# Two blocks of the per-layer input projection moved between the first products of gate and up, with one more tick before a norm

## The chip, the cores and the metric

The kernel runs on one core of a Trainium2 chip. The metric is the device time of one execution in microseconds (us), as a median of several runs. A core has TensorE (PE, matrix products; PEld is its loading of weights), VectorE (DVE), ScalarE (ACT), GpSimd (POOL) and SyncE (SP, which issues most of the transfers between the chip's memory and the core's own). Each engine works through its own list of instructions and waits on semaphores for the others.

## The reference, cut to what matters

The model has two layers over 512 tokens with 1024 channels. Around the change, each layer does this:

```
merged = ga * (ya @ w_br_a) + gb * (yb @ w_br_b) + gc * (yc @ w_br_c)
x = x + merged @ w_o
h = rmsnorm(x, norm_ffn)
x = x + (silu(h @ w_ffn_gate) * (h @ w_ffn_up)) @ w_ffn_down
h = rmsnorm(x, norm_ple)
x = x + sigmoid(h @ w_ple_gate) * (p[i] @ w_ple_in)
```

The change is about `p[i] @ w_ple_in`, the layer's input: `p[i]` is 512 tokens by 256 channels and depends on nothing computed before, so its product may be made at any point of the layer.

## The kernel before, in words

Everything is kept transposed: 128 channels on the partitions, 512 tokens along a row. Each fp32 operand is split into a high and a low part (`split`, L163: ScalarE copies the high part in L144, VectorE subtracts it in L158), and each product is three matmuls (`mm3`, L176: lines L178, L179, L180). `gemm` (L182) makes one block of 128 output channels and fetches its weights through `weights` (L167), whose buffers `wr`, `wh` and `wl` are three each.

The order of TensorE's work is the order in which the program is written. The other engines' orders are made by the framework's scheduler from the program's order, priorities and estimated durations; `weights` and the first loads of the feed-forward stage are given a higher priority, so that they are placed earlier.

Work that is to run a little later on TensorE is written as a generator. `chunk` (L116) counts products of 128 by 128 (three matmuls each, or six of half width in the feed-forward stage), and every fourth one is a tick, at which the waiting generators take a step. `norm` (L207) is such a generator: after `waits[0]` ticks it transposes the sums of squares on TensorE (L214), VectorE reduces them, POOL takes the power, and after `waits[1]` more ticks TensorE turns the result into rows (L227), which ScalarE copies out (`spread`, L255). `main_norm` (L249) starts one; `rows` (L231) then releases what waits for the norm (`ready`, L121).

The stages of a layer that the change touches:

- **Gates and input blocks** (`layer`, L414). The gates of the convolution branch, m = 4 to 7, are made by `gate_b`; between them `input_block` (L1149) makes the first six of the eight blocks of the layer's input: `inputs` (L1138) loads `pT` and splits it into `e` buffers, each block is two products, ScalarE copies it to a `t` buffer, and SP stores it to the memory `pis`. The convolution's last steps are a generator that runs meanwhile; `merge_b` (L745) then reads its result `conv_qk`.
- **w_o** (L865). Eight blocks of the output product, added to x; `halves_in` and `halves_out` build seven combinations of half operands for the next stage (`wo_h`, `wo_qk`, `wo_v`).
- **Gate and up** (`gate_up`, L936). Eleven steps; each makes two blocks of gate and two of up with seven products, called a11, a12, s1, s2, s3, s4 and a22, each 24 matmuls of 256 columns. They share three PSUM banks: x (`ffn_sc`), y (`ffn_tr`) and z (`ffn_av`). Bank x takes a11, s2, s3 and a22 one after the other, each added to what stands in it, and ScalarE copies the bank out between them (`after`, L981, to `ffn_pt` or `ffn_y`). In step 0 the first three products are begun without their last quarter, which needs the last block of w_o; `third` then begins s1, finishes all three and starts their copies. The weights' split for an item (`prep`, `parted`) is written three items ahead.
- **Down** (`down`, in three parts) and, at its end, `main_norm(st[0])` in `ffn` (L1093), with ticks (2, 2).
- **ple** (L1163). For each block m the gate's product, then `rest` multiplies it with the layer's input: for m below `EARLY` (6) read back from `pis` by `embedded`, for m = 6 and 7 of layer 0 made on the spot by `gemm` into `ple_sc` with operands that `inputs` loads just ahead. Layer 1 makes its last two blocks in another way, in `final`, from the same operands. After layer 0's ple the next layer begins with `glu`, whose first two blocks are made as a pair.

Of the kernel before, what the change touches and what calls it, by code (L numbers as in the profile page):

```python
# [12 lines left out]
F32R = mybir.dt.float32r  # L13
I32 = mybir.dt.int32
AF = mybir.ActivationFunctionType
# [5 lines left out]
P = 128  # L21
L = 2
# [4 lines left out]
KD = 8  # L27
# [22 lines left out]
WARM = 10  # L50
BG = dict(glu=2, natten=3, diff=1, gatec=2, branchc=1, gateb=5, mergea=4, mergea2=2)
FIRST = (["v"] * 4 + ["pt"] * 2 + ["y", "b"], ["y"] * 5 + ["pt"] * 2 + ["b"])
EARLY = 6
GAP = 144
AHEAD = dict(sums=12, loads=10)
BACC = dict(dynamic_dma_scratch_size=1024)
# [6 lines left out]
class Net:  # L63
# [350 lines left out]
    def layer(self, i, h, xsrc, xs):  # L414
        self.i, self.h = i, h
        zs, cs = [], []
        self.todo = self.taps(zs, cs)
        self.glu(zs)
        if i == 0:
            self.lambdas()  # L420
        yc, ya, yb = [], [], []
        sn, sd = {}, {}
        self.natten_in(0, sn, yc)
        self.drain(self.renorm)
        self.h = self.hs
# [12 lines left out]
        self.diff_in(3, sd, ya)  # L438
        for m in range(1, KD):
            self.gate_c(acc, m)  # L440
        for m in range(2):
            self.gate_b(gb, m, AF.Copy, None)
        for g in acc + gb:
            self.act(g, g, AF.Sigmoid, table="sigmoid")
        self.branch_c(acc, yc)
        for m in range(2, 4):
            self.gate_b(gb, m, AF.Sigmoid, "sigmoid")
        self.merge_a(ya, acc)
        conv = self.run(self.conv(cs, yb))
        pairs = self.inputs()  # L450
        for m in range(4, KD):
            self.gate_b(gb, m, AF.Sigmoid, "sigmoid")
            for n in ((0, 1), (2,), (3, 4), (5,))[m - 4]:
                self.input_block(pairs, n)
        self.drain(conv)
        mg = self.merge_b(yb, acc, gb)
        x, h = self.w_o(mg, xsrc)
        h = self.ffn(h, x)
        return self.ple(h, x, xs, self.inputs())

    def proj(self, col0, tag="mm"):
        if self.first:
# [399 lines left out]
        self.stt(es[0], es[1], m[:, 5:6], es[0], ALU.mult, ALU.add)  # L862
        return es[0]

    def w_o(self, mg, xsrc):  # L865
        self.phase = "wo"
        xs, st = [], []
        ts = [None] * KP
        for m in range(KD):
            if m % 2 == 0:  # L870
                two = self.parts_of("x", [512], 2)
            xo = two[m % 2]
            self.nc.sync.dma_start(xo, xsrc[m])
            if m == 0:
                both = [self.ps("mm") for _ in range(2)]
                self.pair(both, self.a["w_o"][self.i, 0:2], mg)
            if m < 2:
                ps = both[m]
            else:
                ps = self.ps("mm")  # L880
                self.gemm(ps, self.a["w_o"][self.i, m], mg)
            self.tt(xo, xo, ps, ALU.add)
            if m == KD - 1:
                self.sumsq(m, xo, st)
            if m % 2 == 0:
                ts[m // 2] = self.halves_in(m // 2, xo)
            else:
                self.halves_out(ts[m // 2], xo)
            if m < KD - 1:
                self.sumsq(m, xo, st)  # L890
            xs.append(xo)
        self.main_norm(st[0])
        return xs, [t["out"] for t in ts]

# [38 lines left out]
        self.follow(self.tt(lo, raw, hi.bitcast(F32), ALU.subtract), "dve")  # L933
        return hi, lo

    def gate_up(self, step, ts, mids):  # L936

        nc, w = self.nc, self.a["w_gu"][self.i, step]
        raw, ops, out = {}, {}, {}

        def load(name, src, plus=None, tag="wr"):
            r = raw[name] = self.sb(tag, [P, 1024])
            nc.sync.dma_start(r, src)
            if plus is not None:
                nc.gpsimd.dma_start(r, plus, accum_op=ALU.add)

        def sums():
            load("s1", w[1, 0], w[1, 1], "e" if step % 2 else "kh")
            load("s3", w[1, 0], w[0, 0], "e")

        def loads():
            load("a11", w[0, 0])
            load("a12", w[0, 1])
            load("a22", w[1, 1])

        def prep(name):  # L960
            def fn():
                for s, p, q in (("s2", "s1", "a11"), ("s4", "s2", "a12")):
                    if name == s:
                        raw[s] = self.sb("rp", [P, 1024])
                        self.follow(self.tt(raw[s], raw[p], raw[q], ALU.add), "dve")
                ops[name] = self.parted(raw[name])
            return fn

        def run(bank, name, j, kps=range(KP), first=False):
            if bank not in out:  # L970
                out[bank] = self.ps(dict(x="sc", y="tr", z="av")[bank], (P, 2, 256))
            self.product(out[bank], ops[name], ts, j, kps, first)

        def outputs():
            g = [self.sb("y" if step % 2 else "pt", [P, 2, 512]) for _ in range(2)]
            for u in range(2):
                for v in range(2):
                    out[u, v] = g[u][:, :, 256 * v:256 * v + 256]
            out["g"] = g

        def after(name):  # L981
            if name == "a11":
                outputs()
                self.mark["act"] = self.act(out[0, 0], out["x"], AF.Copy)
            elif name == "a12":
                self.mark["dve"] = self.tt(out[0, 0], out[0, 0], out["y"], ALU.add)
            elif name == "s2":
                self.mark["act"] = self.act(out[0, 1], out["x"], AF.Copy)
            elif name == "s1":
                self.mark["act"] = self.act(out[1, 1], out["z"], AF.Copy, scale=-1.0)  # L990
            elif name == "s3":
                self.mark["dve"] = self.tt(out[1, 1], out[1, 1], out["x"], ALU.subtract)
            elif name == "s4":
                self.mark["dve"] = self.tt(out[0, 1], out[0, 1], out["z"], ALU.add)
                mids[2 * step] = self.mid(2 * step, out["g"][0])
# [12 lines left out]

        order = [("x", "a11", 0), ("y", "a12", 1), ("z", "s1", 3), ("x", "s2", 2), ("x", "s3", 4),
                 ("z", "s4", 6), ("x", "a22", 5)]  # L1010
        if step:
            order[2:4] = order[3:1:-1]
        items = [[prep(o[1]), use(*o)] for o in order]
        if step == 0:
            def third():
                begin(*order[2])()
                for o in order[:3]:
                    run(*o, (KP - 1,))
                    after(o[1])
            items[0][1], items[1][1], items[2][1] = begin(*order[0]), begin(*order[1]), third  # L1020
        return [({0: sums, 4: loads}.get(n), p, u) for n, (p, u) in enumerate(items)]

    def follow(self, i, engine):
# [66 lines left out]
        self.ready(done)  # L1090
        return md

    def ffn(self, ts, x):  # L1093
        self.phase = "ffn"
        i = self.i
        st, hn, mids, items = [], [], {}, []
# [10 lines left out]

        for p, (first, end) in enumerate(PARTS):
            for n in range(first, end):
                items += self.gate_up(n, ts, mids)  # L1110
            items += self.down(p, mids, lambda m, ps, p=p: done(p, m, ps))
        self.mark = {}
        loads = []
# [13 lines left out]
        for n, (_, _, use) in enumerate(items):  # L1127
# [4 lines left out]
            if n + 3 < len(items):  # L1132
                items[n + 3][1]()
                self.p0 = self.tc.cur_priority
        self.main_norm(st[0])
        return hn

    def inputs(self):  # L1138
        self.phase = "pin"
        pairs = []  # L1140
        for k in range(2):
            r = self.sb("t", [P, 512])
# [2 lines left out]
            self.split(hi, lo, r)  # L1145
            pairs.append((hi, lo))
        return pairs

    def input_block(self, pairs, m):  # L1149

# [12 lines left out]
    def ple(self, h, x, xs, pairs):  # L1163
# [3 lines left out]
        hn, st = [], []  # L1167
        for m in range(KD - 2 * last):
            g = self.sb("t", [P, 512])
            if m < EARLY:  # L1170
                pi = self.embedded(m)
            if m != 1:
                pg = self.ps("mm")
# [12 lines left out]
            self.ready(gate)  # L1186
            if last and m == 3:
                self.gains()
            if m >= EARLY:
                pi = self.ps("sc")  # L1190
                self.gemm(pi, self.a["w_pi"][i, m], pairs)

            def rest(m=m, pi=pi, g=g):
                self.tt(g, g, pi, ALU.mult)
                self.tt(x[m], x[m], g, ALU.add)
# [241 lines left out]
```

## Time and profile before

| | us |
|---|---|
| median of 3 runs (lowest to highest) | 1801.88 (1801.6 to 1803.25) |
| the profiled execution | 1801.18 |
| its span, first to last instruction | 1799.4 |
| TensorE busy in the span | 1780.7 |
| VectorE busy | 1380.7 |
| ScalarE busy | 893.1 |
| POOL busy | 64.1 |

The granted TensorE clock is 0.998 of full speed over the span. In the timeline each row gives a start, a length, the engine, the line, the operation with the tile that it writes and those that it reads, and in brackets the engine's idle time before it with what ended that. Matmuls are pipelined: those of 512 columns are listed 0.39 us long but start 0.23 us apart, those of 256 columns 0.28 us long and 0.12 us apart. So a stretch in which TensorE lost time is best read from the starts.

### The profile page before, as it was taken

Reading aid. Unit: us, or ns where it says so; the run is one execution under the profiler, and the core shown is the slowest. Engines: PE = TensorE matmul, PEld = TensorE weight load, DVE = VectorE, ACT = ScalarE, POOL = GpSimd, SP = SyncE. Lnnn points to the kernel's source line nnn. Section 1 sums busy time; section 2 is a strip of 40 time slices with the busy share of each in tenths; the row PEclk is TensorE's granted clock in tenths of the full one; section 3 lists DMA queues with packets and bytes.
Section 4 is the critical chain, followed back from the end, with each engine's and each line's share of the span. In section 5 each row is a group of like instructions: output and inputs, shape, how many; then the busy total and the mean of one; then the engine's idle time right before and its main releaser. Section 6 shows DMA issues by size and latency. Waiting matters only on the chain. (4 is left out here: it accounts for less than half of the span.)

```text
span 1799.4 us, 27361 instructions
## 1 busy us (share of the span) xinstructions
PE 1780.7 (99%) x10404; PEld 1573.4 (87%) x10404; DVE 1380.7 (77%) x2140; ACT 893.1 (50%) x1495; POOL 64.1 (4%) x102
## 2 busy tenths in 40 slices
PE   9999999999999999999999999999999999999998
PEld 7888888888889899898888888888888998998987
DVE  7878887897877577577777878878887775765776
ACT  5467455325565245255545755553255552543554
POOL 0000000000001000000000000000000100000000
PEclk9999999999999999999999999999999999999999
DMA  5566561325646466253437656523374662764432
GB/s 199 165 189 164 150 161 42 103 91 177 198 111 187 138 155 186 81 145 115 157 123 188 187 153 161 128 62 100 97 225 129 156 186 82 192 175 112 115 109 94
DMA packets 98099, 255.98 MB, mean 142 GB/s; under 512 B 12976, under 2 KB 18480, under 8 KB 97968
## 3 DMA queue, kind: packets, MB, share of 16 engines
q1 hardware_dynamic: 90480, 229.62, 41.8%
q0 software_dynamic: 6336, 23.07, 7.3%
q8 instruction: 82, 1.34, 0.3%
q10 hardware_dynamic: 1152, 1.55, 0.3%
q14 instruction: 49, 0.40, 0.1%
HBM read 215.39 MB, written 7.34 MB: 124 GB/s over the span
## 5 line engine op out<-in xcount | busy, mean ns | idle before, releaser
L144 ACT ACTIVATE ffn_wh<-ffn_wr 128x1024 fp32r<-128x1024 f32 (+1 forms) x114 | 117.3, 1029 | 184.9 <-PE ffn_mm L179 101.8
L161 DVE SCALAR_TENSOR_TENSOR conv_z<-glu_z,pre_par,conv_z 128x512 f32<-128x512 f32 x240 | 179.5, 748 | 2.9
L158 DVE TENSOR_TENSOR ffn_wl<-ffn_wr,ffn_wh 128x1024 fp32r<-128x1024 f32 (+1 forms) x114 | 135.0, 1184 | 47.2 <-ACT ffn_wh L144 46.7
L1040 PE MATMUL ffn_sc<-wo_h,ffn_wh 128*128 128x256 f32 x704 | 130.8, 284 | 4.4 <-ACT ffn_pt L144 4.4
L1040 PEld LDWEIGHTS ffn_sc<-wo_h,ffn_wh 128*128 128x128 f32 x704 | 110.1, 192 | 5.8 <-ACT ffn_pt L144 5.3
L1040 PE MATMUL ffn_sc<-wo_h,ffn_wl 128*128 128x256 f32 x352 | 99.6, 283 | 0.0
L178 PE MATMUL ffn_mm<-ffn_z,ffn_wh 128*128 128x512 f32 x240 | 93.4, 389 | 0.0
L179 PE MATMUL ffn_mm<-ffn_z,ffn_wh 128*128 128x512 f32 x240 | 93.4, 389 | 0.0
L180 PE MATMUL ffn_mm<-ffn_z,ffn_wl 128*128 128x512 f32 x240 | 93.4, 389 | 0.0
L158 DVE TENSOR_TENSOR ffn_t<-ffn_mm,wo_r 128x512 f32<-128x512 f32 x48 | 33.1, 689 | 70.6 <-PE ffn_mm L180 70.6
L158 DVE TENSOR_TENSOR ffn_wl<-ffn_rp,ffn_wh 128x1024 fp32r<-128x1024 f32 x44 | 53.8, 1223 | 30.1 <-ACT ffn_wh L144 30.1
L144 ACT ACTIVATE mergea_wh<-mergea_wr 128x1024 fp32r<-128x1024 f32 (+1 forms) x32 | 27.1, 846 | 96.8 <-PE mergea_mm L179 70.8
L1040 PEld LDWEIGHTS ffn_sc<-wo_h,ffn_wl 128*128 128x128 f32 x352 | 67.5, 192 | 0.0
L1040 PE MATMUL ffn_sc<-wo_qk,ffn_wh 128*128 128x256 f32 x352 | 67.1, 283 | 0.0
L1040 PE MATMUL ffn_sc<-wo_v,ffn_wh 128*128 128x256 f32 x352 | 67.1, 283 | 0.0
L1040 PE MATMUL ffn_av<-wo_h,ffn_wh 128*128 128x256 f32 x352 | 65.3, 283 | 0.0
L144 ACT ACTIVATE ffn_wh<-ffn_rp 128x1024 fp32r<-128x1024 f32 x44 | 46.4, 1055 | 30.6 <-PE ffn_mm L179 17.5
L1040 PEld LDWEIGHTS ffn_sc<-wo_qk,ffn_wh 128*128 128x128 f32 x352 | 54.9, 192 | 0.0
L1040 PEld LDWEIGHTS ffn_av<-wo_h,ffn_wh 128*128 128x128 f32 x352 | 54.9, 192 | 0.0
L1040 PEld LDWEIGHTS ffn_sc<-wo_v,ffn_wh 128*128 128x128 f32 x352 | 54.9, 192 | 0.0
L180 PEld LDWEIGHTS ffn_mm<-ffn_z,ffn_wl 128*128 128x128 f32 x240 | 45.1, 188 | 9.5
L178 PEld LDWEIGHTS ffn_mm<-ffn_z,ffn_wh 128*128 128x128 f32 x240 | 45.1, 188 | 9.2
(666 smaller groups left out, 5786.4 us busy)
## 6 DMA issues: line engine op xcount, KB each, us to landing
ffn_wr<-w_gu SPq DMA_DIRECT2D x66, 512.0 KB, 4.3
ffn_e<-w_gu SPq DMA_DIRECT2D x32, 512.0 KB, 3.6
ffn_e<-w_gu POOLq DMA_DIRECT2D x32, 512.0 KB, 7.8
ffn_wr<-w_fd SPq DMA_DIRECT2D x32, 512.0 KB, 4.5
natten_wr<-w_in SPq DMA_DIRECT2D x16, 512.0 KB, 4.3
natten_b<-bias SPq DMA_DIRECT2D x32, 256.0 KB, 2.9
diff_wr<-w_in SPq DMA_DIRECT2D x16, 512.0 KB, 3.7
gatec_wr<-w_in SPq DMA_DIRECT2D x16, 512.0 KB, 3.8
```

The source lines that it names most:

```text
L144: i = self.nc.scalar.activation(out, in_, func, **kw)
L158: return self.nc.vector.tensor_tensor(out, a, b, op)
L161: return self.nc.vector.scalar_tensor_tensor(out, a, s, b, op0, op1)
L178: mm(out, wh, ah, start=first, stop=False)
L179: mm(out, wh, al, start=False, stop=False)
L180: mm(out, wl, ah, start=False, stop=last)
L1040: mm(bank[:, u], w[:, u, kp], t, start=begin and n == 0, stop=False, skip_group_check=True)
```

## The change

- In step 0 of gate and up, one block of the layer's input is made after `third` (that is, after a11, a12 and s1) and another after s2. They use an `mm` bank, ScalarE copies each one out, and SP stores it to `pis`. Layer 0 makes its blocks 6 and 7 there, layer 1 its blocks 4 and 5.
- Their operands are loaded and split during w_o, after its blocks 1 and 2: twice `pT` (into `a` and `b` buffers) and twice a block of `w_pi` (into `r` and `a` buffers).
- In layer 1 the gates m = 4 to 7 of the convolution branch are followed by one input block each (0, 1, 2, 3), six blocks before. Layer 0 keeps its order.
- ple reads every block from `pis`; its two products on the spot are gone, and layer 0 no longer calls `inputs` ahead of it.
- The norm behind down gets ticks (3, 2).

```diff
-EARLY = 6
...
         for m in range(4, KD):
             self.gate_b(gb, m, AF.Sigmoid, "sigmoid")
-            for n in ((0, 1), (2,), (3, 4), (5,))[m - 4]:
+            for n in (((0, 1), (2,), (3, 4), (5,)), ((0,), (1,), (2,), (3,)))[i][m - 4]:
                 self.input_block(pairs, n)
         self.drain(conv)
         mg = self.merge_b(yb, acc, gb)
-        x, h = self.w_o(mg, xsrc)
-        h = self.ffn(h, x)
-        return self.ple(h, x, xs, self.inputs())
+        extra = self.extra_inputs(range(6 - 2 * i, 8 - 2 * i))
+        x, h = self.w_o(mg, xsrc, extra)
+        h = self.ffn(h, x, extra)
+        return self.ple(h, x, xs, self.inputs() if i == L - 1 else None)
...
             xs.append(xo)
+            if m in (1, 2):
+                extra["pair"](m - 1)
         self.main_norm(st[0])
...
                 for o in order[:3]:
                     run(*o, (KP - 1,))
                     after(o[1])
-            items[0][1], items[1][1], items[2][1] = begin(*order[0]), begin(*order[1]), third
+                extra["block"](0)
+
+            def fourth():
+                use(*order[3])()
+                extra["block"](1)
+
+            items[0][1], items[1][1] = begin(*order[0]), begin(*order[1])
+            items[2][1], items[3][1] = third, fourth
...
-        self.main_norm(st[0])
+        self.main_norm(st[0], (3, 2))
...
+    def extra_inputs(self, ms):
+        nc, i = self.nc, self.i
+        pairs, blocks = [None, None], {}
+
+        def pair(k):
+            ph, self.phase = self.phase, "pin"
+            r = self.sb("t", [P, 512])
+            nc.sync.dma_start(r, self.a["pT"][i, k])
+            hi, lo = [self.sb("ab"[k], [P, 512], F32R) for _ in range(2)]
+            self.split(hi, lo, r)
+            pairs[k] = hi, lo
+            w = self.sb("t", [P, 256])
+            nc.sync.dma_start(w, self.a["w_pi"][i, ms[k]])
+            hi, lo = self.sb("a" if k else "r", [P, 256], F32R), self.sb("r", [P, 256], F32R)
+            self.split(hi, lo, w)
+            blocks[k] = hi, lo
+            self.phase = ph
+
+        def block(n):
+            ph, self.phase = self.phase, "pin"
+            ps = self.ps("mm")
+            hi, lo = blocks[n]
+            for k in range(2):
+                s = slice(k * P, k * P + P)
+                self.mm3(ps, hi[:, s], lo[:, s], *pairs[k], k == 0, k == 1)
+            o = self.sb("t", [P, 512])
+            self.act(o, ps, AF.Copy)
+            nc.sync.dma_start(self.pis[ms[n]], o)
+            self.phase = ph
+
+        return dict(pair=pair, block=block)
...
-            if m < EARLY:
+            if m < KD - 2 * last:
                 pi = self.embedded(m)
...
-            if m >= EARLY:
-                pi = self.ps("sc")
-                self.gemm(pi, self.a["w_pi"][i, m], pairs)
-
```

`block` calls `mm3` directly, without `chunk`, so the two blocks count for no tick; the products that they replace did count, four chunks in each layer.

More of the change, by code (lines that the diff above doesn't have):

```diff
@@ L863, in probs, with w_o @@
         return es[0]
-    def w_o(self, mg, xsrc):
+    def w_o(self, mg, xsrc, extra):
         self.phase = "wo"
@@ L934, in parted, with gate_up @@
         return hi, lo
-    def gate_up(self, step, ts, mids):
+    def gate_up(self, step, ts, mids, extra):
         nc, w = self.nc, self.a["w_gu"][self.i, step]
@@ L1091, in mid, with ffn @@
         return md
-    def ffn(self, ts, x):
+    def ffn(self, ts, x, extra):
         self.phase = "ffn"
@@ L1109, in ffn @@
             for n in range(first, end):
-                items += self.gate_up(n, ts, mids)
+                items += self.gate_up(n, ts, mids, extra)
             items += self.down(p, mids, lambda m, ps, p=p: done(p, m, ps))
```

## The prediction

> **What bounds the kernel now.** I read the page first, for the span and the engines' shares.
>
> ```profile
> span 1799.4 us, 27361 instructions
> PE 1780.7 (99%) x10404; PEld 1573.4 (87%) x10404; DVE 1380.7 (77%) x2140; ACT 893.1 (50%) x1495; POOL 64.1 (4%) x102
> ```
>
> TensorE is busy in 1780.7 of 1799.4 us. The change keeps its number of matmuls, so all that a new order can win lies in the 18.7 us that remain. Next come TensorE's waits.
>
> ```profile
> PE ffn_sc L1040 <- ACT ffn_pt L144: 4.4, 4, 1.2
> ```
>
> ```profile
> PE ffn_tr L214 <- DVE ffn_ss L158: 1.6, 2, 0.8
> ```
>
> Two groups touch the change: four waits of a gate-and-up product for ScalarE's copy, and two of the norm behind down for its sum of squares. The TensorE timeline of layer 0 shows where the first group stands.
>
> ```profile
> 514.91 0.28 PE L1040 MATMUL ffn_av<-wo_v,ffn_wl 128*128 128x256 f32 x1
> 516.21 0.39 PE L1040 MATMUL ffn_sc<-wo_h,ffn_wh 128*128 128x256 f32 x1 [1.02 <-ACT ffn_pt L144]
> ...
> 519.19 0.60 PE L227 MATMUL wo_tr<-pre_ident,wo_rc 128*128 128x128 f32 x4
> 520.97 0.39 PE L1040 MATMUL ffn_sc<-wo_h,ffn_wh 128*128 128x256 f32 x1 [1.19 <-ACT ffn_pt L144]
> ```
>
> The first wait is ahead of s2, the second ahead of s3, both in step 0: bank x must be copied out before the next product is added to it. ScalarE's timeline says why the copies are late.
>
> ```profile
> 513.67 1.06 ACT L144 ACTIVATE ffn_wh<-ffn_rp 128x1024 fp32r<-128x1024 f32 x1 [2.65 <-PE ffn_sc L1040]
> 514.63 1.04 ACT L144 ACTIVATE ffn_wh<-ffn_e 128x1024 fp32r<-128x1024 f32 x1
> 515.58 0.58 ACT L144 ACTIVATE ffn_pt<-ffn_sc 128x512 f32<-128x512 f32 x1
> ...
> 518.89 1.06 ACT L144 ACTIVATE ffn_wh<-ffn_rp 128x1024 fp32r<-128x1024 f32 x1 [2.25 <-DVE ffn_rp L158]
> 519.85 0.58 ACT L144 ACTIVATE wo_r<-wo_tr 128x512 f32<-128x512 f32 x1
> 520.33 0.59 ACT L144 ACTIVATE ffn_pt<-ffn_sc 128x512 f32<-128x512 f32 x1
> ```
>
> The first copy (515.58) stands behind the splits of s2's and s3's weights, which themselves had to wait for a11's buffers; the second (520.33) behind s4's split and the norm's rows. Layer 1 repeats it to the digit.
>
> ```profile
> 1404.65 0.51 PE L1040 MATMUL ffn_sc<-wo_h,ffn_wh 128*128 128x256 f32 x2 [1.02 <-ACT ffn_pt L144]
> ```
>
> ```profile
> 1409.41 0.51 PE L1040 MATMUL ffn_sc<-wo_h,ffn_wh 128*128 128x256 f32 x2 [1.19 <-ACT ffn_pt L144]
> ```
>
> The second group, in layer 0 (its twin in layer 1 waits as long, by the total of 1.6 in 2):
>
> ```profile
> 856.26 0.39 PE L180 MATMUL ple_mm<-ffn_qk,ple_wl 128*128 128x512 f32 x1
> 857.42 0.66 PE L214 MATMUL ffn_tr<-pre_ident,ffn_ss 128*128 128x128 f32 x4 [0.77 <-DVE ffn_ss L158]
> ```
>
> **The change part by part.** I count lost time from start to start. Matmuls of 512 columns start 0.227 us apart, so after 856.26 the next was due at 856.49 and came at 857.42: 0.93 lost. Those of 256 columns start 0.12 apart: s2 was due at 515.03 and came at 516.21, 1.18 lost. For s3 and the cost of a block two more rows each are needed.
>
> ```profile
> 907.41 0.60 PE L214 MATMUL ple_tr<-pre_ident,ple_ss 128*128 128x128 f32 x4
> 907.77 0.48 PE L178 MATMUL glu_mm<-ple_pt,glu_wh 128*128 128x512 f32 x1
> ```
>
> ```profile
> 897.88 0.39 PE L178 MATMUL ple_sc<-pin_e,ple_wh 128*128 128x512 f32 x1
> ```
>
> ```profile
> 899.24 0.39 PE L178 MATMUL glu_mm<-ple_y,glu_wh 128*128 128x512 f32 x1
> ```
>
> Four transposes take 0.36, so s3 was due at 519.55 and came at 520.97: 1.42 lost. One input block takes 1.36.
>
> *The blocks.* They leave places without a wait: removing two saves 2.72 per layer. In step 0, block 0 runs from 515.03 to 516.39. The copy ends at 515.58 + 0.58 = 516.16, so s2 no longer waits; it starts 0.18 later than before. The transposes move from 519.19 to 519.37; block 1 runs from 519.73 to 521.09. What ScalarE does after the transposes also moves by 0.18, so s2's copy lets s3 start at 521.15, against 520.97. The step is 0.18 later and holds 2.72 of moved work: 2.54 per layer, **5.08** in both.
>
> The Trainium skill ("Perfetto Trace Analysis", Tensor Engine Instruction) says that a matmul's end in the profile is estimated, not observed. The rows agree, since matmuls listed 0.39 long start 0.23 apart. By the idle column the two groups hold 4.4 + 1.6 = 6.0 us, by the starts 2 x (1.18 + 1.42 + 0.93) = 7.06.
>
> *What the blocks bring to other engines.*
>
> ```profile
> L144 ACT ACTIVATE pin_t<-pin_sc x12: 573/579/591, 420.5 to 1329.7; 128x512 f32<-128x512 f32 x12
> ```
>
> ```profile
> L1143 SPq DMA_DIRECT2D pin_t<-pT x8: 424/426/539, 403.5 to 1742.7; - x8
> L144 ACT ACTIVATE pin_e<-pin_t x8: 616/632/636, 409.2 to 1746.6; 128x512 fp32r<-128x512 f32 x8
> L158 DVE TENSOR_TENSOR pin_e<-pin_t,pin_e x8: 684/686/694, 410.7 to 1748.0; 128x512 fp32r<-128x512 f32 x8
> ```
>
> ```profile
> L144 ACT ACTIVATE pin_wh<-pin_wr x12: 397/418/420, 406.2 to 1321.1; 128x256 fp32r<-128x256 f32 x12
> L158 DVE TENSOR_TENSOR pin_wl<-pin_wr,pin_wh x12: 416/423/426, 406.6 to 1321.9; 128x256 fp32r<-128x256 f32 x12
> ```
>
> A block's copy takes 0.58 of ScalarE. Block 0's falls into the 2.25 idle before 518.89. Block 1's can start at about 521.3 and pushes the next split; that split's product, a22, comes only after s3 and s4, about 5.8 us later. In w_o the operands cost ScalarE 2 x (0.632 + 0.418) = 2.10 and VectorE 2 x (0.686 + 0.423) = 2.22 per layer.
>
> ```profile
> 471.99 1.06 ACT L144 ACTIVATE wo_wh<-wo_wr 128x1024 fp32r<-128x1024 f32 x1 [3.81 <-PE wo_mm L179]
> ```
>
> ```profile
> 472.17 0.69 DVE L158 TENSOR_TENSOR wo_x<-wo_x,wo_mm 128x512 f32<-128x512 f32 x1 [3.27 <-PE wo_mm L180]
> ```
>
> Both engines sit idle longer than that at the very place, and TensorE has no wait in w_o. I take 0; with the cover gone it is at most 2.10 + 2.22 = 4.32 per layer, one after the other.
>
> *SP's queue.* In w_o it gains four loads per layer, in step 0 two stores that wait for ScalarE; whatever is issued behind them waits too.
>
> ```profile
> 517.15 0.33 SPq L947 DMA_DIRECT2D ffn_e<-w_gu  x1
> ```
>
> ```profile
> 524.07 1.06 ACT L144 ACTIVATE ffn_wh<-ffn_wr 128x1024 fp32r<-128x1024 f32 x1 [2.21 <-issue]
> ```
>
> A load issued in step 0 feeds splits like that at 524.07, for a product at about 529.6 (520.97 and three products of 24 x 0.12). If block 1's store (ready at about 521.8) stood ahead of it, some 3 us of slack would go, and nothing else. I take 0. ple's two extra reads per layer 0 are issued three blocks ahead, like the other six.
>
> *The later norm.* One tick is twelve matmuls, 2.72 us. The sum of squares was 0.93 late, so that wait goes: **1.86** for both layers. But the rows come later.
>
> ```profile
> 863.40 0.60 PE L227 MATMUL ffn_tr<-pre_ident,ffn_rc 128*128 128x128 f32 x4
> ```
>
> ```profile
> 869.32 0.39 PE L178 MATMUL ple_mm<-ffn_qk,ple_wh 128*128 128x512 f32 x1
> ```
>
> ple's fourth block (869.32, now 868.39) needs the bank of the first, which VectorE frees once the rows are there. The transposes come at 863.40 - 0.93 + 2.72 = 865.19; spread (0.58) and VectorE's product (0.69) end by about 867.2. 1.2 us are left: 0. Bounded from above by a split (1.06) and one of VectorE's own (1.22) in the way, it would lose 1.1 per layer.
>
> *Layer 1's gates.* Two blocks fewer bring `merge_b` 2.72 closer to the convolution's last steps, whose ticks come after as many matmuls as before.
>
> ```profile
> 1328.14 0.69 DVE L158 TENSOR_TENSOR conv_qk<-conv_z,conv_qk 128x512 fp32r<-128x512 f32 x1 [0.70 <-ACT conv_qk L144]
> ```
>
> ```profile
> 1329.13 0.39 PE L178 MATMUL mergeb_mm<-conv_qk,mergeb_wh 128*128 128x512 f32 x1
> ```
>
> The last operand is ready at 1328.83; the eleventh matmul, the first that reads it, would come at 1326.41 + 10 x 0.227 = 1328.68. I take **0.15** lost; it is 0 if VectorE, freed of two small splits, is earlier, and 2.72 if the chain slips as far as the blocks did.
>
> *The sum:* 5.08 + 1.86 - 0.15 = 6.8. The profiled execution took 1801.18 (its span and 1.78 around it), so 1794.4; the median of the runs is 0.70 above it: **1795.1**.
>
> **The rivals.** *A: s3 still waits.* If block 0's copy gets behind s4's split, s2's copy is 0.58 later; with a22's split (1.06) ahead as well 1.64. Twice that gives 1796.3 to 1798.4. Against it: the copy is written before that split and ScalarE is idle then. The Trainium skill ("TensorE: Matmul & The Clock Gate", Architectural detail) says that ScalarE's queue is strictly first in, first out; by that rule the whole 0.58 would count, and the rows above, each copy right behind the split ahead of it, agree.
>
> *B: a later stage gives back.* `merge_b` waits the whole 2.72, or ple's fourth block twice 1.1: 1797.3 to 1797.7.
>
> *C: the operands are not hidden.* 4.32 per layer: up to 1803.7, half of it about 1799.4. Idle time at the place speaks against it.
>
> *D: the waits move behind the blocks*, since what is awaited is later than the copy. Only the norm's 1.86 is won: 1800.0. Against it: TensorE starts 0.05 after each copy ends.
>
> *E: slower.* The four operand loads get behind the load of 517.15 in SP's queue, as their priority is plain and that of the weights is raised. Four issues of 0.43, then 3.7 us to land and a split of 0.63 + 0.69 put the last operand at about 523.3, where block 0 is due at 515.03: 8.3 later, with all of TensorE behind it, in both layers. 1795.1 + 16.6 = 1811.7. It decides from 3.4 us of delay per layer on. Against it: the loads of x in w_o have the same plain priority and were issued in time.
>
> ```profile
> pin_t<-pT SPq DMA_DIRECT2D x8, 256.0 KB, 3.7
> ```
>
> **How the numbers follow.** Forecast 0.58, A 0.14, B 0.06, C 0.06, D 0.06, E 0.10. Forecast, A and B hold 0.78, so the range takes in D at 1800.0; its low end, 1794.0, is 1801.88 less the 7.06 and 0.8, half the spread of the three runs. 0.2% is 3.6 us, about what a measurement of this kernel can tell from no change: faster (below 1798.3) is the forecast and nearly all of A and B, 0.77; same C, D and a rest, 0.12; slower E and a rest of C, 0.11.
>
> **What would show it.** Right: TensorE's waits hold no `ffn_sc <- ffn_pt` above 0.2 and no `ffn_tr <- ffn_ss`; `pin_mm` matmuls stand right ahead of s2 and of s3; `merge_b` and ple have no new wait. A: a copy of `pin_t` between s4's split and s2's copy. C: a wait in w_o or at a11's last quarter. D: the same 1.0 and 1.2 behind the blocks. E: a wait of `pin_mm` for its operands. The forecast fails if a stage that I left out lost its order.

## The result, and the profile after

The changed kernel takes 1795.05 us (median of 12 runs, 1791.86 to 1798.74) beside 1800.54 for the kernel before (12 runs, 1797.74 to 1803.65). The ratio is 0.997, with a 95% interval of 0.9961 to 0.998, so 3.6 to 7.0 us were won. The profiled execution took 1793.92. From here on "before" and "after" are the two kernels. In the line numbers of after, `mm3` is L177 to L179, ScalarE's copies are L143, VectorE's operations L157 and L160, a norm's transposes L213 (sums) and L226 (rows), and the products of gate and up L1049.

The page of after: the span, and the engines.

```profile
span 1792.1 us, 27370 instructions
PE 1778.6 (99%) x10404; PEld 1571.3 (88%) x10404; DVE 1381.7 (77%) x2142; ACT 895.0 (50%) x1499; POOL 63.5 (4%) x102
```

TensorE's waits in after, by what it waited for (us in total, times, longest). The two groups that the prediction started from, `ffn_sc <- ffn_pt` with 4.4 and `ffn_tr <- ffn_ss` with 1.6, are not in the list. Two others are new:

```profile
PE ple_tr L213 <- DVE ple_ss L157: 1.0, 1, 1.0
...
PE conv_tr L226 <- POOL conv_rc L222: 0.4, 1, 0.4
```

The TensorE timeline of step 0 of gate and up in layer 0: the last matmul of a block of the layer's input, and what follows it.

```profile
513.36 0.40 PE L179 MATMUL pin_mm<-pin_b,pin_r 128*128 128x512 f32 x1
513.60 0.39 PE L1049 MATMUL ffn_sc<-wo_h,ffn_wh 128*128 128x256 f32 x2
...
516.46 0.60 PE L226 MATMUL wo_tr<-pre_ident,wo_rc 128*128 128x128 f32 x4
...
518.06 0.39 PE L179 MATMUL pin_mm<-pin_b,pin_r 128*128 128x512 f32 x1
518.29 0.39 PE L1049 MATMUL ffn_sc<-wo_h,ffn_wh 128*128 128x256 f32 x2
```

s2 (513.60) and s3 (518.29) start 0.24 and 0.23 behind the matmul ahead of them, the plain distance: neither waits. ScalarE's timeline of the same stretch shows by how much:

```profile
512.75 0.58 ACT L143 ACTIVATE ffn_pt<-ffn_sc 128x512 f32<-128x512 f32 x1
...
513.80 0.60 ACT L143 ACTIVATE pin_t<-pin_mm 128x512 f32<-128x512 f32 x1
516.05 1.06 ACT L143 ACTIVATE ffn_wh<-ffn_rp 128x1024 fp32r<-128x1024 f32 x1 [1.66 <-DVE ffn_rp L157]
517.02 0.58 ACT L143 ACTIVATE ffn_pt<-ffn_sc 128x512 f32<-128x512 f32 x1
517.50 0.59 ACT L143 ACTIVATE wo_r<-wo_tr 128x512 f32<-128x512 f32 x1
```

Bank x is copied out by 513.33 for s2 and by 517.60 for s3. The second copy (517.02) now stands ahead of the copy of the norm's rows (517.50); in before it stood behind it. The scheduler swapped the two.

The new waits stand in TensorE's timeline of the next layer's `glu` and of layer 1's gates:

```profile
901.08 0.39 PE L179 MATMUL glu_mm<-ple_pt,glu_wl 128*128 128x512 f32 x1
902.43 0.63 PE L213 MATMUL ple_tr<-pre_ident,ple_ss 128*128 128x128 f32 x4 [0.96 <-DVE ple_ss L157]
```

```profile
1310.05 0.39 PE L179 MATMUL gateb_mm<-ple_h,gateb_wl 128*128 128x512 f32 x1
1310.87 0.65 PE L226 MATMUL conv_tr<-pre_ident,conv_rc 128*128 128x128 f32 x4 [0.43 <-POOL conv_rc L222]
```

A matmul of 512 columns takes 0.227 from start to start, so the two cost 902.43 - 901.31 = 1.12 and 1310.87 - 1310.28 = 0.59.

The whole change can be laid out as a table of stretches, each from TensorE's first matmul of one stage to its first of another. "w_o, step 0" ends at the first matmul of down, and the last row ends at TensorE's last transposes.

| stretch (starts in before; in after) | before | after | difference | forecast |
|---|---|---|---|---|
| start to w_o, layer 0 (to 462.45; 459.62) | | | -2.83 | 0 |
| w_o, step 0, gate and up, layer 0 (to 590.18; 587.39) | 127.73 | 127.77 | +0.04 | +0.18 |
| on to ple, layer 0 (to 851.05; 848.65) | 260.87 | 261.26 | +0.39 | 0 |
| ple, layer 0 (to 899.24; 893.15) | 48.19 | 44.50 | -3.69 | -3.65 |
| glu (to 944.01; 939.03) | 44.77 | 45.88 | +1.11 | 0 |
| on to merge_a, layer 1 (to 1232.09; 1227.32) | 288.08 | 288.29 | +0.21 | 0 |
| merge_a, gates, layer 1 (to 1329.13; 1322.26) | 97.04 | 94.94 | -2.10 | -2.57 |
| merge_b, layer 1 (to 1350.89; 1344.02) | 21.76 | 21.76 | 0 | 0 |
| w_o, step 0, gate and up, layer 1 (to 1478.63; 1471.80) | 127.74 | 127.78 | +0.04 | +0.18 |
| on to ple, layer 1 (to 1739.49; 1733.04) | 260.86 | 261.24 | +0.38 | 0 |
| ple, layer 1 (to 1792.57; 1785.15) | 53.08 | 52.11 | -0.97 | -0.93 |

The forecast is the prediction's: 0.18 per step 0; 2.72 + 0.93 in ple; 2.72 - 0.15 in the gates, where its 0.15 stood at merge_b. Four rows (-2.83, +0.39, +0.21, +0.38) are stretches in which the matmuls and their order did not change. The runs below show for three of them that they vary between executions of one kernel. For +0.21 it is not shown: two profiles of the changed kernel have 288.29 and 288.23 there, and the one of before is the lowest of all. The rest is -5.57, against the forecast's -6.79. Behind the last row the span goes on for 6.83 us in before and 6.98 in after; every profile with the moved blocks has about as much more, and the prediction had no term for it.

### The profile page after: what moved, and what is told of

Its sections match the earlier page's. It is cut to its first block, busy times and chain, and to the rows that moved or that the text cites. A ratio compares the mean times of both kernels' runs of the same rounds, so it can differ in the third digit from the quotient of the medians.

```text
span 1792.1 us, 27370 instructions
## 1 busy us (share of the span) xinstructions
PE 1778.6 (99%) x10404; PEld 1571.3 (88%) x10404; DVE 1381.7 (77%) x2142; ACT 895.0 (50%) x1499; POOL 63.5 (4%) x102
## 5 line engine op out<-in xcount | busy, mean ns | idle before, releaser
L143 ACT ACTIVATE ffn_wh<-ffn_wr 128x1024 fp32r<-128x1024 f32 (+1 forms) x114 | 117.3, 1029 | 184.1 <-PE ffn_mm L178 99.5
L160 DVE SCALAR_TENSOR_TENSOR conv_z<-glu_z,pre_par,conv_z 128x512 f32<-128x512 f32 x240 | 179.2, 747 | 2.9
L157 DVE TENSOR_TENSOR ffn_wl<-ffn_wr,ffn_wh 128x1024 fp32r<-128x1024 f32 (+1 forms) x114 | 134.9, 1183 | 49.9 <-ACT ffn_wh L143 49.5
L1049 PE MATMUL ffn_sc<-wo_h,ffn_wh 128*128 128x256 f32 x704 | 130.4, 283 | 0.0
L1049 PEld LDWEIGHTS ffn_sc<-wo_h,ffn_wh 128*128 128x128 f32 x704 | 110.4, 192 | 0.8
L1049 PE MATMUL ffn_sc<-wo_h,ffn_wl 128*128 128x256 f32 x352 | 99.6, 283 | 0.0
L177 PE MATMUL ffn_mm<-ffn_z,ffn_wh 128*128 128x512 f32 x240 | 93.4, 389 | 0.0
L179 PE MATMUL ffn_mm<-ffn_z,ffn_wl 128*128 128x512 f32 x240 | 93.4, 389 | 0.0
L157 DVE TENSOR_TENSOR ffn_t<-ffn_mm,wo_r 128x512 f32<-128x512 f32 x48 | 33.1, 689 | 67.8 <-PE ffn_mm L179 67.8
L157 DVE TENSOR_TENSOR ffn_wl<-ffn_rp,ffn_wh 128x1024 fp32r<-128x1024 f32 x44 | 53.7, 1221 | 30.3 <-ACT ffn_wh L143 30.3
L143 ACT ACTIVATE mergea_wh<-mergea_wr 128x1024 fp32r<-128x1024 f32 (+1 forms) x32 | 27.1, 846 | 96.8 <-PE mergea_mm L178 70.8
L1049 PEld LDWEIGHTS ffn_sc<-wo_h,ffn_wl 128*128 128x128 f32 x352 | 67.5, 192 | 0.0
L1049 PE MATMUL ffn_sc<-wo_qk,ffn_wh 128*128 128x256 f32 x352 | 67.1, 283 | 0.0
L1049 PE MATMUL ffn_sc<-wo_v,ffn_wh 128*128 128x256 f32 x352 | 67.1, 283 | 0.0
L1049 PE MATMUL ffn_av<-wo_h,ffn_wh 128*128 128x256 f32 x352 | 65.3, 283 | 0.0
L143 ACT ACTIVATE ffn_wh<-ffn_rp 128x1024 fp32r<-128x1024 f32 x44 | 46.4, 1055 | 29.6 <-PE ffn_mm L178 17.5
L1049 PEld LDWEIGHTS ffn_sc<-wo_qk,ffn_wh 128*128 128x128 f32 x352 | 54.9, 192 | 0.0
L1049 PEld LDWEIGHTS ffn_av<-wo_h,ffn_wh 128*128 128x128 f32 x352 | 54.9, 192 | 0.0
L1049 PEld LDWEIGHTS ffn_sc<-wo_v,ffn_wh 128*128 128x128 f32 x352 | 54.9, 192 | 0.0
L179 PEld LDWEIGHTS ffn_mm<-ffn_z,ffn_wl 128*128 128x128 f32 x240 | 45.1, 188 | 9.3
```

What stands on the lines that cost most here:

```text
L143: i = self.nc.scalar.activation(out, in_, func, **kw)
L157: return self.nc.vector.tensor_tensor(out, a, b, op)
L160: return self.nc.vector.scalar_tensor_tensor(out, a, s, b, op0, op1)
L177: mm(out, wh, ah, start=first, stop=False)
L179: mm(out, wl, ah, start=False, stop=last)
L1049: mm(bank[:, u], w[:, u, kp], t, start=begin and n == 0, stop=False, skip_group_check=True)
```

## The experiments

Two questions were open. **First**, does the place of the blocks win what step 0 shows, or is it that they left other places? **Second**, where do the 1.12 and 0.59 come from? For the first of these waits there were two theories: the rows of the norm behind down, one tick later, make VectorE late in ple; or the two removed blocks, 2.72 us of TensorE, were the cover. All times of stretches are read as in the table.

**The blocks elsewhere.** The two blocks were put behind s3 and s4:

```diff
-                extra["block"](0)
...
-            items[2][1], items[3][1] = third, fourth
+            items[2][1], items[4][1], items[5][1] = third, later(4), later(5)
```

Here `later(n)` makes product n and then block n - 4.

> The changed kernel with its two blocks after s3 and after s4 of step 0, where TensorE has no wait, instead of after s1 and after s2. The matmuls are the same. By the prediction (the place is what counts): the waits ahead of s2 and s3 return, 2.6 us per layer, 5.2 in all above the changed kernel, about 1800.2. Rival (what counts is that the blocks left ple and the gates): no more than 0.5 above the changed kernel.

Measured: 1801.12, ratio to before 0.9999 (0.999 to 1.0009). The runs show no gain any more. TensorE's waits of this kernel:

```profile
PE ffn_sc L1050 <- ACT ffn_pt L143: 3.4, 4, 1.0
```

The step 0 stretch takes 130.02 and 130.03, so 2.25 per layer above after, 4.5 in all. The forecast of 5.2 was a little too high because the copy that s3 waits for kept its new place ahead of the rows' copy, and the wait came back as 0.70 by the idle column, not 1.19. The place is what counts.

**The blocks left out.**

```diff
-                self.mm3(ps, hi[:, s], lo[:, s], *pairs[k], k == 0, k == 1)
...
-            self.act(o, ps, AF.Copy)
+            self.act(o, pairs[n][0].bitcast(F32), AF.Copy)
```

> The changed kernel without the twelve matmuls of each of the four moved blocks: ScalarE copies the first operand out in their place, so the layer's input is wrong in four blocks (blocks 6 and 7 of layer 0, 4 and 5 of layer 1). Loads, splits, copies and stores all stay. If the blocks only fill waits, as the prediction has it: the waits of s2 and s3 for bank x come back at 1.2 to 1.4 us each, start to start, and the time is 0.2 to 0.4 us per layer below the changed kernel (2 x 1.36 of work less 2.60 of waits that return, with step 0's own 0.04). Rival (the waits would be gone without the blocks, since ScalarE's order has changed): 2.7 us per layer, 5.4 in all, below the changed kernel.

Measured: 1795.01, ratio 0.9971 (0.9959 to 0.9983), no different from after. TensorE's waits of this kernel:

```profile
PE ffn_sc L1049 <- ACT ffn_pt L143: 4.4, 4, 1.2
```

With nothing to fill them the four waits are back to the digit, and the step 0 stretch takes 127.73 and 127.74. With two blocks in it, it takes 127.77 and 127.78. So 2.72 us of TensorE's work cost 0.04 there. That is less than the 0.2 to 0.4 per layer expected.

**One part at a time.** First the change with ticks (2, 2) behind down:

```diff
-        self.main_norm(st[0], (3, 2))
+        self.main_norm(st[0])
```

> The change without its later norm: the norm behind down has its ticks (2, 2) again, all else is as after. Both theories expect the wait of the transposes for VectorE's sum of squares back in both layers (0.93 us each, start to start) and no ffn_sc <- ffn_pt wait. Theory 1 (ple's VectorE work runs late in the changed kernel because the norm's rows come one tick later): the new wait of 1.12 us of ple's own norm at 902.43 is gone, so about 0.7 us above the changed kernel, near 1795.8. Theory 2 (it is late because the two blocks of the layer's input left ple, 2.72 us of TensorE work that covered VectorE): that wait stays, about 1.9 us above the changed kernel, near 1796.9. The two times lie within the noise of the runs; TensorE's waits in ple tell them apart.

Measured: 1796.26, ratio 0.9977 (0.9968 to 0.9986). ple takes 45.48 and 53.10, so 0.98 and 0.99 above after, and TensorE waits as in before:

```profile
PE ffn_tr L213 <- DVE ffn_ss L157: 1.6, 2, 0.8
```

The wait in `glu` is gone: the stretch takes 44.76, as in before. That was theory 1's mark. Then the kernel before with the later tick alone:

```diff
-        self.main_norm(st[0])
+        self.main_norm(st[0], (3, 2))
```

> The kernel before with one edit of the change alone: ticks (3, 2) for the norm behind down. Prediction's term: 1.86 us below the kernel before, and the four ffn_sc <- ffn_pt waits of step 0 stay at 4.4 us by the idle column. Theory 1 (rows one tick later make ple's VectorE work late): a wait of ple's norm for VectorE of up to 1.1 us appears ahead of the next layer's glu, so only 0.8 us below before. Theory 2 (the removed blocks' cover): no such wait, because here ple still makes two blocks on the spot.

Measured: 1798.06, ratio 0.9984 (0.9975 to 0.9992). ple takes 47.22 and 52.11, 0.97 less in each layer, and `glu` takes 44.76: no wait there either, which was theory 2's mark. So the wait of 1.12 needs both parts, and neither theory as stated is enough.

**What the two parts do together.** If TensorE simply comes 2.72 + 0.93 earlier and VectorE does not, less late rows would mend only a part of it. The test gives the rows back their old place and keeps the late transposes:

```diff
-        self.main_norm(st[0], (3, 2))
+        self.main_norm(st[0], (3, 1))
```

> The changed kernel with ticks (3, 1) for the norm behind down: the transposes of the sums stay late, the rows come back to their old place. The runs with one part each show the wait of ple's own norm (1.11 us) in neither, so it needs both the 0.93 us of the norm and the 2.72 us of the two blocks. Theory 1 (margin: TensorE arrives 3.65 us earlier, VectorE's last sum of squares does not): rows one tick earlier bring VectorE's order of before back, the sum ends as in the run without the later norm (53.25 us after ple's start) and the transposes are due at 52.7, so the wait shrinks to 0.7; 0.4 us below the changed kernel. Theory 2 (late rows alone make VectorE late): the wait goes, 1.1 below. Price to both: reduction, scaling and power must fit into one tick (2.72 of 3.2 us in ple's own norm); if a split of 1.22 us gets between them, up to 0.8 us lost per layer.

Measured: 1793.81, ratio 0.9962 (0.9949 to 0.9975). `glu` takes 44.76: the whole wait is gone, where theory 1 expected 0.7 of it to stay. ple keeps its 44.49 and 52.11, so the norm's chain fits into one tick. VectorE's timeline for the last two blocks of ple, first in after:

```profile
893.44 0.68 DVE L157 TENSOR_TENSOR ple_t<-ple_mm,ffn_r 128x512 f32<-128x512 f32 x1
894.27 1.23 DVE L157 TENSOR_TENSOR glu_wl<-glu_wr,glu_wh 128x1024 fp32r<-128x1024 f32 x1
895.41 0.68 DVE L157 TENSOR_TENSOR ple_ss<-ple_ss,ple_t 128x512 f32<-128x512 f32 x1
896.01 0.68 DVE L157 TENSOR_TENSOR ple_t<-ple_t,ple_a 128x512 f32<-128x512 f32 x1
...
897.34 0.68 DVE L157 TENSOR_TENSOR ple_t<-ple_mm,ffn_r 128x512 f32<-128x512 f32 x1
898.22 0.75 DVE L160 SCALAR_TENSOR_TENSOR ple_pt<-wo_x,pre_par,ple_pt 128x512 fp32r<-128x512 f32 x1 [0.19 <-ACT ple_pt L143]
898.88 0.68 DVE L157 TENSOR_TENSOR ple_ss<-ple_ss,ple_t 128x512 f32<-128x512 f32 x1
899.49 0.68 DVE L157 TENSOR_TENSOR ple_t<-ple_t,ple_a 128x512 f32<-128x512 f32 x1
...
901.59 0.69 DVE L157 TENSOR_TENSOR ple_ss<-ple_ss,ple_t 128x512 f32<-128x512 f32 x1 [0.70 <-ACT ple_t L143]
```

and with (3, 1):

```profile
891.82 0.68 DVE L157 TENSOR_TENSOR ple_t<-ple_mm,ffn_r 128x512 f32<-128x512 f32 x1
893.26 0.69 DVE L157 TENSOR_TENSOR ple_t<-ple_t,ple_a 128x512 f32<-128x512 f32 x1 [0.76 <-ACT ple_t L143]
893.99 0.69 DVE L157 TENSOR_TENSOR wo_x<-wo_x,ple_t 128x512 f32<-128x512 f32 x1
894.85 1.23 DVE L157 TENSOR_TENSOR glu_wl<-glu_wr,glu_wh 128x1024 fp32r<-128x1024 f32 x1 [0.17 <-ACT glu_wh L143]
...
897.26 0.68 DVE L157 TENSOR_TENSOR ple_t<-ple_mm,ffn_r 128x512 f32<-128x512 f32 x1
898.70 0.69 DVE L157 TENSOR_TENSOR ple_t<-ple_t,ple_a 128x512 f32<-128x512 f32 x1 [0.76 <-ACT ple_t L143]
...
900.82 0.69 DVE L157 TENSOR_TENSOR ple_ss<-ple_ss,ple_t 128x512 f32<-128x512 f32 x1 [0.70 <-ACT ple_t L143]
```

In after, the split of the next weights (1.23) and the sum of the block ahead stand between a block's two products (893.44 and 896.01). In the last block the operand and the sum of the block ahead stand there (898.22, 898.88). ScalarE's list has its part of the split ahead of the block's sigmoid in the same way. With (3, 1) the split stands behind the block's work, and the last block's two products wait only for the sigmoid. From the last matmul of ple's gates to the last sum that is 8.67 us in after:

```profile
892.92 0.39 PE L179 MATMUL ple_mm<-ffn_v,ple_wl 128*128 128x512 f32 x1
```

and 7.32 with (3, 1) (893.50 to 900.82). The run with the norm alone is as late as after, 8.70 from the same matmul to its last sum (903.79), which ends at 904.48. But there an input block still stands between ple's gates and `glu` (of the two, only the last stands behind all the gates), and the transposes come only at 904.84.

```profile
895.09 0.39 PE L180 MATMUL ple_mm<-ffn_v,ple_wl 128*128 128x512 f32 x1
...
904.84 0.38 PE L214 MATMUL ple_tr<-pre_ident,ple_ss 128*128 128x128 f32 x2
```

Counted from the last matmul of ple's gates in layer 0, five profiles give the whole account (us):

| | last sum starts | ends (0.69) | transposes due | left |
|---|---|---|---|---|
| before | 6.66 | 7.35 | 9.75 | 2.40 |
| later norm alone | 8.70 | 9.39 | 9.75 | 0.36 |
| blocks alone, ticks (2, 2) | 7.31 | 8.00 | 8.39 | 0.39 |
| blocks, ticks (3, 1) | 7.32 | 8.01 | 8.39 | 0.38 |
| after, ticks (3, 2) | 8.67 | 9.36 | 8.39 | -0.97 |

So late rows make VectorE 1.35 later at the end of ple (2.04 where the blocks are still there). The removed blocks bring the transposes 1.36 nearer and leave VectorE 0.65 later. Either part alone fits into the 2.4 that before had, both together do not. This also corrects theory 1 in the last test. Its 0.7 was counted from ple's start, in a run that still had the 0.98 wait of the norm behind down inside ple. Counted from the gates, 7.31 leaves no wait, so the test does not refute theory 1.

What stays open is how the late rows delay the end. They come 2.72 later after ple's start (14.09 against 11.37 us), VectorE's first product with them comes 1.73 later, and its order is another. No run keeps the late rows and gives back the order, so the share of each is not shown.

**Moving the consumer instead.** If VectorE is late, giving ple's own norm a later tick should not help for long. Two forms of it:

```diff
-        self.main_norm(st[0], (3, 2), x=x)
+        self.main_norm(st[0], (4, 1), x=x)
```

> The changed kernel with ticks (4, 1) instead of (3, 2) for the norm behind layer 0's ple: the transposes one tick later, the rows where they were. VectorE's order then has a split of glu's weights (1.23 us, ready at 905.35) ahead of the reduction and another between the reduction and the scaling. If VectorE's order counts: reduction at 906.5, second split to 908.4, scaling 0.17, POOL 1.01, so the rows' transposes are due at 906.75 and come at about 909.6: 2.9 us of wait in place of 1.11, 1.8 above the changed kernel. Rival (only the place of the transposes counts): the wait goes, 1.1 below.

Measured: 1795.16, ratio 0.9973 (0.996 to 0.9986); `glu` takes 46.33, 0.45 above after. TensorE's timeline:

```profile
902.17 0.50 PE L178 MATMUL glu_mm<-ple_b,glu_wh 128*128 128x512 f32 x1 [0.29 <-DVE ple_b L160]
904.14 0.60 PE L213 MATMUL ple_tr<-pre_ident,ple_ss 128*128 128x128 f32 x4
907.98 0.65 PE L226 MATMUL ple_tr<-pre_ident,ple_rc 128*128 128x128 f32 x4 [0.50 <-POOL ple_rc L222]
```

The transposes of the sums don't wait, but what VectorE makes next, the last operand `ple_b`, is late now, and so are the rows, whose chain runs behind two splits. Neither theory had the size: the rows were 0.65 late by the starts, not 2.9. Counted from `glu`'s start (892.30 here, 893.15 in after) they came 0.77 earlier than the expectation had it, since the splits did, and were due 1.43 later, since the expectation left out the transposes and the wait for `ple_b`.

```diff
-        self.main_norm(st[0], (3, 2), x=x)
+        self.main_norm(st[0], (4, 2), x=x)
```

> The changed kernel with ticks (4, 2) instead of (3, 2) for the norm behind layer 0's ple. The transposes are due one tick later, 904.03 instead of 901.31, behind VectorE's last sum at 902.28: the wait of 1.11 us goes. The rows come 2.72 us later than they were due, 1.6 later than they came. Theory 1 (margin): 1.1 below the changed kernel. Rival: what waits for the rows (glu's gates and the release of its banks) is late instead, and TensorE loses up to 1.6 us there: 0.5 above.

Measured: 1799.14, ratio 0.9988 (0.9976 to 1.0); `glu` takes 49.79, 3.91 above after. Both theories missed it:

```profile
913.19 0.60 PE L226 MATMUL ple_tr<-pre_ident,ple_rc 128*128 128x128 f32 x4
916.17 0.79 PE L177 MATMUL glu_mm<-ple_y,glu_wh 128*128 128x512 f32 x1 [2.38 <-DVE glu_t L157]
916.77 0.63 PE L178 MATMUL glu_mm<-ple_y,glu_wh 128*128 128x512 f32 x1
917.19 0.63 PE L179 MATMUL glu_mm<-ple_y,glu_wl 128*128 128x512 f32 x1
...
919.87 0.39 PE L177 MATMUL glu_mm<-ple_y,glu_wh 128*128 128x512 f32 x1
```

The release of a bank needs the rows and is late by 2.62: four transposes from 913.19 end their turn at 913.55, and the next matmul came at 916.17. The rival had the kind of wait, but priced it at 1.6. ScalarE's copy of the rows (914.17) stands behind a split (913.20) here, and VectorE's product that releases the bank (915.44) behind another (914.29). Behind it nine matmuls take 3.70 where 9 x 0.227 = 2.04 is plain: another 1.66 (919.87 - 916.17 less 2.04), of which more at the end.

**The gates.** The 0.59 has the same look. VectorE's timeline in after:

```profile
1307.74 0.69 DVE L215 TENSOR_REDUCE conv_sm<-conv_tr 128x4 f32<-128x512 f32 x1 [1.10 <-PE conv_tr L213]
1308.35 1.21 DVE L157 TENSOR_TENSOR gateb_wl<-gateb_wr,gateb_wh 128x1024 fp32r<-128x1024 f32 x1
1309.48 0.16 DVE L218 TENSOR_SCALAR conv_sm<-conv_sm 128x4 f32<-128x4 f32 x1
```

A split stands between the reduction of the convolution's sums and their scaling, which POOL and then TensorE wait for. In before the two stand next to each other (1312.68 and 1313.40). The blocks were spread in another way:

```diff
-            for n in (((0, 1), (2,), (3, 4), (5,)), ((0,), (1,), (2,), (3,)))[i][m - 4]:
+            for n in (((0, 1), (2,), (3, 4), (5,)), ((0, 1), (2,), (3,), ()))[i][m - 4]:
```

> The changed kernel with layer 1's four remaining input blocks behind gates 4, 4, 5 and 6 instead of one behind each of the four. The convolution's last wait (0.59 us start to start at 1310.87, TensorE for POOL) comes in the changed kernel from VectorE's order, in which a split of the gates' weights (1.21 us) stands between the reduction of the sums and their scaling. Theory: with the blocks spread so, the two stand next to each other again and the stretch from merge_a to merge_b gets 0.6 us shorter (94.94 to 94.3); the time 0.6 us below the changed kernel, within the noise of the runs. Rival (the two removed blocks themselves took the cover from the convolution's chain): the wait stays or moves, 94.9 or more.

Measured: 1793.17, ratio 0.996 (0.9945 to 0.9976). The stretch takes 94.32, and the list of waits holds no `conv_tr`:

```profile
1308.15 0.69 DVE L215 TENSOR_REDUCE conv_sm<-conv_tr 128x4 f32<-128x512 f32 x1
1308.87 0.17 DVE L218 TENSOR_SCALAR conv_sm<-conv_sm 128x4 f32<-128x4 f32 x1
1310.28 1.23 DVE L157 TENSOR_TENSOR gateb_wl<-gateb_wr,gateb_wh 128x1024 fp32r<-128x1024 f32 x1 [1.23 <-ACT gateb_wh L143]
```

97.04 - 94.32 = 2.72: the two removed blocks now bring all they held. The rival is excluded by TensorE's own places too: the rows are due 82.96 us after merge_a's first matmul in before, in after and here, since the blocks count for ticks. The removal took no cover from this wait; what differs is VectorE's order. (In the runs with ticks (2, 2) and (3, 1) behind down the split stands there as in after, and the stretch takes 95.13 and 95.12.)

**Both mends, beside the changed kernel again.** One kernel has (3, 1) and the other spread together:

```diff
-        self.main_norm(st[0], (3, 2))
+        self.main_norm(st[0], (3, 1))
...
-            for n in (((0, 1), (2,), (3, 4), (5,)), ((0,), (1,), (2,), (3,)))[i][m - 4]:
+            for n in (((0, 1), (2,), (3, 4), (5,)), ((0, 1), (2,), (3,), ()))[i][m - 4]:
```

The changed kernel ran once more, unaltered, on the same chip.

> Both mends together: ticks (3, 1) for the norm behind down, and layer 1's input blocks behind gates 4, 4, 5 and 6. Each alone took away its own wait (1.13 us of ple's norm; 0.62 us of the convolution's). Theory (the two lie in different stages and add): no ple_tr and no conv_tr wait, from w_o of layer 0 to the end 1325.53 - 1.13 - 0.62 - 0.4 (the slow transfer that only the profile of the changed kernel has, twice 0.4) = 1323.0 us; about 1793.3 or 1.75 below the changed kernel, 7.3 below the kernel before. Rival (one mend moves the other's order): one of the two waits comes back, 1323.6 to 1324.1.

> The changed kernel itself, unaltered, beside the mended one on the same chip. The waits of ple's norm (1.1 us) and of the convolution's norm (0.6 us) are the kernel's own and stay; the two losses of 0.4 us in the stretches of gate and up, behind a split that waits for a transfer, vary from one execution to the next and need not show in the same places.

Measured: 1793.58, ratio 0.9956 (0.9944 to 0.9968), and for the changed kernel 1795.53, ratio 0.9965 (0.9953 to 0.9977). The mended one is the fastest kernel of this case by its stretches: from w_o of layer 0 to the end it takes 1323.07 (1323.0 expected), `glu` 44.76 and the gates 94.42 (94.32 with the spread alone). The changed kernel repeats 45.91 and 94.96. The intervals of the two ratios overlap, so the runs alone don't tell these kernels apart; the traces do, with 1.15 + 0.54 us.

The second run of the changed kernel also settles three of the four rows of the table that no edit explains. "On to ple" in layer 0 was 0.39 above before in its first profile and 1.21 in the second (262.08), and in layer 1 0.38 and 0.12; in the mended kernel it is 0 in both. So it is the execution, not the edit. The start up to w_o ends at 459.62 in one profile of the changed kernel and at 460.97 in the other.

## Why the prediction was right or wrong

- **The blocks in step 0: right, and a little better.** s2 and s3 wait no more in either layer, and the step is 0.04 later, not 0.18, since the scheduler took s2's copy out from behind the rows' copy. That is 0.28 more in both layers than the 5.08.
- **"Removing two saves 2.72 per layer": the step that failed.** It held in ple itself (48.19 to 44.50, with the norm's 0.97), but the stretch behind gave 1.11 back, and layer 1's gates saved 2.10. The prediction rightly found no waits at these places. It did not ask how much time VectorE had in hand at the end of ple, nor whether its order in the gates would stay.
- **"The rows come later ... 1.2 us are left: 0".** The working looked at ple's fourth block, which indeed does not wait. It did not ask what later rows do to the rest of VectorE's work in ple, up to the last sum of squares, nor to the order that the scheduler makes for it. VectorE's timeline of before has it:

```profile
904.32 0.69 DVE L158 TENSOR_TENSOR ple_ss<-ple_ss,ple_t 128x512 f32<-128x512 f32 x1 [0.70 <-ACT ple_t L144]
```

  It ends at 905.01, and the transposes came at 907.41, 2.4 us later. Of the 3.65 us taken out of TensorE's time ahead of them only one block, 1.36, stood between ple's last gate and the transposes; the mended kernel takes out the same 3.65 and does not wait. VectorE's own delay of 2.01 (6.66 to 8.67) used up the rest. The row of 907.41 was in the prediction, as the price of four transposes.
- **The later norm: right.** 1.86 was forecast, 0.97 per layer came in ple.
- **merge_b, 0.15: the wrong place and size.** merge_b doesn't wait, not even with the other spread: VectorE has its last operand ready 0.44 earlier than in before (96.30 against 96.74 us after merge_a's first matmul), the prediction's condition for 0. The price came some 11 us earlier, in the convolution's norm: 0.59 to 0.62, because VectorE's order changed there. The prediction took the convolution's chain as slipping in whole or not at all.
- **The rivals.** A (s3 still waits), C (operands not hidden), D (the waits move behind the blocks) and E (SP's queue) did not happen: the loads of the moved operands are issued at 471.88 to 480.03, no wait stands in w_o. B, a later stage that gives back, did happen, though at neither of the places it named, and with 1.7 instead of 2.2 to 2.7 us. (By E's own terms its last operand would come at 523.8, not 523.3.) The prediction's last sentence, that it fails if a stage left out lost its order, names what happened.

The gain of the runs, 5.5 (3.6 to 7.0), agrees with the 5.57 of the stretches (5.42 with the 0.15 at the end) and holds the forecast's 6.8 too. That the forecast time of 1795.1 was hit to 0.05 is luck: it was set against a median of 1801.88 from three runs, and twelve runs gave 1800.54, which makes up for the gain of 1.3 that did not come.

## What to carry to other kernels

Work put into an engine's waits is free only at the place of the waits: the same blocks two products later cost 2.25 per layer. When work is taken out, find for each later meeting of two engines how long the other side has been done. Compare that with what was taken out between the other side's last input and the meeting, and with what makes the other side itself later; here 2.4 stood against 1.36 and 2.01. And where a scheduler orders an engine, a small shift of one step can put a long operation into the middle of a short chain: the loss in the gates was one split of 1.2 us between a reduction and its scaling. Both losses went when the step that had shifted was moved again; moving the consumer only moved the first of them.

## What the runs showed of the hardware that was not expected

TensorE's clock fell after waits much shorter than a stage. The profile of the kernel with ticks (4, 2), by stretches (the granted clock is the third figure from the end):

```profile
912.00:916.00 4.00, 1.79 (x10) 1.24 (x9) 1.71 (x2) 1.54 (x2) 0.00 (x0) 1.00 0.68 246
916.00:920.00 4.00, 3.83 (x10) 3.06 (x11) 4.00 (x9) 2.59 (x4) 0.00 (x0) 0.57 0.45 131
```

After one wait of 2.38 us the granted clock was 0.57, and matmuls of 512 columns started 0.43 apart for 3.2 us. The same happens in some executions in layer 0's neighbourhood attention, which waits twice for transfers at about 76 to 79 us. The mended kernel's profile:

```profile
77.00:80.00 3.00, 1.26 (x6) 1.02 (x7) 1.04 (x5) 0.44 (x2) 0.00 (x0) 0.99 1.04 234
80.00:83.00 3.00, 3.00 (x8) 2.32 (x8) 0.49 (x3) 2.00 (x6) 0.00 (x0) 0.50 0.50 125
```

Two waits there (1.47 and 1.14 by the idle column) are followed by a clock of 0.50. Of the twelve profiles four show this drop, before among them, and after does not. The length of the waits alone does not decide: before's two were 0.65 and 0.88 and the clock fell, while 0.96 and 0.78 in the run with the blocks left out passed without a drop. From the first of those two products (`natten_sc`) to the next transposes before took 9.27 us (77.08 to 86.35) and after 7.61 (76.88 to 84.49): 1.66 of the 2.83 in the first row of the table. Why the transfers are later in some executions stays open.

The Trainium skill ("TensorE: Matmul & The Clock Gate", Part 1: The HAM clock gate) says that the clock halves after an idle window of about 3.4 us and comes back after a busy one as long, and that the windows run free. The half clock and the 3.2 us agree; the waits that brought it on were shorter, 2.38 us alone, or 2.6 and 1.5 in two parts.
